# Squared-ReLU MLP of a two-layer decoder trunk: from column 1024 on, the up projection takes u's high and low part in one 512-column product

## Chip, cores and metric

One core of a Trainium2 chip. The metric is device time in microseconds (us) of one execution, lower is better.

## What is computed

Two decoder layers over 256 tokens of width 1024, all in f32. The change touches the second half of each layer, the MLP; from the reference:

```python
u = x * (1.0 + sc2) + sh2
h = jnp.square(jax.nn.relu(u @ w_up[l])) @ w_down[l]      # w_up 1024 x 4096, w_down 4096 x 1024
x = layer_norm(DN_ALPHA * x + (1.0 + gt2) * h, ln_ffn_g[l], ln_ffn_b[l])
```

`sc2`, `sh2`, `gt2` and their like for the first half come from `c_act @ w_ada[l] + b_ada[l]`, one row vector for all tokens.

## The kernel before

**Two-part products.** Every f32 operand of a large product is cut into a rounded high part and the rest (`wh`, `wl`; `uh`, `ul`; `hh`, `hl`), and a product is three matmuls into the same PSUM bank: high by high, high by low, low by high (`rowmm`, lines 312 to 316; `colmm`, lines 318 to 322). The first operand of a matmul call is the one that TensorE holds, the second streams through.

**Weights.** `Stream` (lines 101 to 147) loads all weights in units of 512 KB in the order of the list `units` (lines 278 to 300), with SP's queue into 5 raw tiles. ScalarE rounds a unit into `wh` (line 121), VectorE subtracts for `wl` (line 122). Eight units are live; the split of a new unit goes into the tiles of the unit that `done(i)` has just given up, so ScalarE's `wh` waits for TensorE's last product with that unit.

**The MLP** (`ffn`, lines 999 to 1057). Columns 0 to 1023 of the up projection go token by token row (`row_phase`). From column 1024 on it is done transposed, in blocks of 512 columns, b = 2 to 7: `col_group` holds a 128 x 128 piece of the weights and streams 256 tokens, 8 k-tiles x 4 column pieces x 3 products of 256 columns into the banks `ua` and `ub`; `relu2_split` then takes each bank out (ReLU, square, rounding on ScalarE, rest on VectorE) into `hid[b]`. Between two blocks stand 4 units of the down projection of the block before, 48 products of 512 columns into the four banks `acc`, which are called `d` in the profile. The last 8 units of the down projection follow, 48 products for each half of the tokens; behind each half come the norm and the next layer's `u`.

**Work beside it.** `Background.step()` is called after each unit and moves on, above all, the vectors from `w_ada`: on VectorE `adaa += ada * ccol` over 8 loads of 512 KB (`ada_dve_gate`, `ada_dve_cols`), three load tiles in turn. A gate vector is then spread over all rows (`gate_rows`, lines 436 to 449): ScalarE rounds (`gh`), VectorE subtracts (`gl`), TensorE multiplies with ones (`gtb`, line 445 with `gh`, line 446 with `gl`), for each half of 512 columns. In layer 0's MLP the gate rows of that layer and all of the next layer's shifts and scales run this way, in layer 1's only its last gate, in the first 12 us.

The order of instructions on each engine is fixed when the kernel is built, by a scheduler that starts from the order of the code; each engine works its list in order.

## Time and profile before

| | |
|---|---|
| median of 3 runs | 754.73 us (753.99 to 755.18) |
| the profiled execution's own time | 755.1 us |
| its span in the profile | 753.2 us |
| busy: TensorE / weight load / VectorE / ScalarE | 97% / 84% / 79% / 60% |
| granted TensorE clock, mean | 0.994 |

The profile is of one execution. Its span ends about 1.9 us short of that execution's own time. Busy shares are means over stages with different limits. PE is TensorE's products, PEld its weight loads, DVE VectorE, ACT ScalarE, SP the engine that issues the loads.

### The profile page before, as it was taken

Reading aid. Unit: us, or ns where it says so; the run is one execution under the profiler, and the core shown is the slowest. Engines: PE = TensorE matmul, PEld = TensorE weight load, DVE = VectorE, ACT = ScalarE, POOL = GpSimd, SP = SyncE. Lnnn points to the kernel's source line nnn. Section 1 sums busy time; section 2 is a strip of 40 time slices with the busy share of each in tenths; the row PEclk is TensorE's granted clock in tenths of the full one; section 3 lists DMA queues with packets and bytes.
Section 4 is the critical chain, followed back from the end, with each engine's and each line's share of the span. In section 5 each row is a group of like instructions: output and inputs, shape, how many; then the busy total and the mean of one; then the engine's idle time right before and its main releaser. Section 6 shows DMA issues by size and latency. Waiting matters only on the chain.

```text
span 753.2 us, 12252 instructions
## 1 busy us (share of the span) xinstructions
PE 733.7 (97%) x4648; PEld 633.3 (84%) x4648; DVE 592.7 (79%) x870; ACT 448.5 (60%) x737; POOL 15.0 (2%) x37
## 2 busy tenths in 40 slices
PE   6999999999999999999999999999999999999995
PEld 4667788899888999889877888899988889998885
DVE  2448999999798988688889999997879884454437
ACT  3439898875476654555454985976457565445530
POOL 0000000010000000000000000001000000000001
PEclk9999999999999999999999999999999999999998
DMA  9998889677368998899786744446546885555501
GB/s 278 310 326 318 312 306 321 230 255 247 132 228 276 398 395 319 313 319 343 265 304 218 268 131 161 142 146 212 193 158 221 292 308 179 194 196 189 176 1 56
DMA packets 81562, 181.40 MB, mean 241 GB/s; under 512 B 6264, under 2 KB 24544, under 8 KB 81504
## 3 DMA queue, kind: packets, MB, share of 16 engines
q1 hardware_dynamic: 81440, 180.61, 69.8%
q8 instruction: 36, 0.59, 0.3%
q14 instruction: 22, 0.18, 0.1%
q10 hardware_dynamic: 64, 0.02, 0.0%
HBM read 179.56 MB, written 1.05 MB: 240 GB/s over the span
## 4 chain that ended last, share of the span: by engine, by line
PE 84%; DMA 6%; DVE 4%; ACT 2%; issue 2%; SPq 1%; POOL 1%; POOLq 0%; DVEq 0%; ACTq 0%
PE d L315 6%; PE d L316 6%; PE d L314 6%; DMA ada<-in_w_ada_dram 4%; PE ua L320 3%; PE ua L322 3%; PE ua L321 3%; PE ub L321 3%; PE ub L320 3%; PE ub L322 3%; PE ga L320 2%; PE gb L320 2%; PE ga L321 2%; PE gb L321 2%; PE ga L322 2%; PE gb L322 2%
## 5 line engine op out<-in xcount | busy, mean ns | idle before, releaser
L121 ACT ACTIVATE wh<-w 128x1024 fp32r<-128x1024 f32 x232 | 244.7, 1059 | 190.5 <-PE d L316 58.3
L122 DVE TENSOR_TENSOR wl<-w,wh 128x1024 fp32r<-128x1024 f32 x232 | 281.7, 1224 | 87.3 <-ACT wh L121 86.5
L314 PE MATMUL d<-wh,hh 128*128 128x512 f32 (+1 forms) x256 | 99.6, 389 | 0.0
L315 PE MATMUL d<-wl,hh 128*128 128x512 f32 (+1 forms) x256 | 98.9, 386 | 0.0
L316 PE MATMUL d<-wh,hl 128*128 128x512 f32 (+1 forms) x256 | 98.9, 386 | 0.0
L604 DVE SCALAR_TENSOR_TENSOR acc<-hconv,vc,acc 128x256 f32<-128x256 f32 x150 | 65.8, 497 | 0.0
L314 PEld LDWEIGHTS d<-wh,hh 128*128 128x128 f32 x256 | 48.1, 188 | 10.1 <-ACT relusq L992 0.8
L316 PEld LDWEIGHTS d<-wh,hl 128*128 128x128 f32 x256 | 48.1, 188 | 9.8
L315 PEld LDWEIGHTS d<-wl,hh 128*128 128x128 f32 x256 | 48.1, 188 | 9.2
L320 PE MATMUL ua<-uh,wh 128*128 128x256 f32 x192 | 54.5, 284 | 0.0
L322 PE MATMUL ua<-uh,wl 128*128 128x256 f32 x192 | 54.3, 283 | 0.0
L320 PE MATMUL ub<-uh,wh 128*128 128x256 f32 x192 | 54.3, 283 | 0.0
L321 PE MATMUL ub<-ul,wh 128*128 128x256 f32 x192 | 54.3, 283 | 0.0
L322 PE MATMUL ub<-uh,wl 128*128 128x256 f32 x192 | 54.3, 283 | 0.0
L321 PE MATMUL ua<-ul,wh 128*128 128x256 f32 x192 | 54.3, 283 | 0.0
L600 ACT ACTIVATE tap<-hconv,vc 128x256 f32<-128x256 f32 x90 | 39.3, 501 | 0.1
L495 DVE SCALAR_TENSOR_TENSOR adaa<-ada,ccol,adaa 128x1024 f32<-128x1024 f32 x28 | 35.8, 1280 | 3.7 <-DMA ada<-in_w_ada_dram 3.6
L320 PEld LDWEIGHTS ua<-uh,wh 128*128 128x128 f32 x192 | 36.8, 192 | 1.3 <-issue 0.8
L320 PE MATMUL ga<-uh,wh 128*128 128x256 f32 x128 | 37.5, 293 | 0.0
L321 PEld LDWEIGHTS ua<-ul,wh 128*128 128x128 f32 x192 | 36.8, 192 | 0.4
L320 PE MATMUL gb<-uh,wh 128*128 128x256 f32 x128 | 36.9, 288 | 0.0
L320 PEld LDWEIGHTS ub<-uh,wh 128*128 128x128 f32 x192 | 36.9, 192 | 0.0
(274 smaller groups left out, 1704.4 us busy)
## 6 DMA issues: line engine op xcount, KB each, us to landing
ada<-in_w_ada_dram SPq DMA_DIRECT2D x80, 512.0 KB, 4.9
w<-in_w_in_dram SPq DMA_DIRECT2D x72, 512.0 KB, 4.8
w<-in_w_up_dram SPq DMA_DIRECT2D x64, 512.0 KB, 4.8
w<-in_w_down_dram SPq DMA_DIRECT2D x64, 512.0 KB, 5.2
ada<-in_w_ada_dram SPq DMA_DIRECT2D x32, 256.0 KB, 6.4
w<-in_w_out_dram SPq DMA_DIRECT2D x16, 512.0 KB, 4.3
w<-in_w_attn_br_dram SPq DMA_DIRECT2D x8, 512.0 KB
w<-in_w_conv_pw_dram SPq DMA_DIRECT2D x8, 512.0 KB, 4.8
```

Source lines behind the costliest of these rows:

```text
L121: a = nc.scalar.activation(wh, w, AF.Copy)
L122: b = nc.vector.tensor_tensor(wl, w, wh.bitcast(F32), op=ALU.subtract)
L314: nc.tensor.matmul(b, lh, wh, start=first, stop=False, skip_group_check=True)
L315: nc.tensor.matmul(b, lh, wl, start=False, stop=False, skip_group_check=True)
L316: return nc.tensor.matmul(b, ll, wh, start=False, stop=last, skip_group_check=True)
L320: nc.tensor.matmul(b, wh, rh, start=first, stop=False, skip_group_check=True)
L321: nc.tensor.matmul(b, wh, rl, start=False, stop=False, skip_group_check=True)
L322: nc.tensor.matmul(b, wl, rh, start=False, stop=last, skip_group_check=True)
L495: nc.vector.scalar_tensor_tensor(acc, src, ccol[:, j:j + 1], acc, op0=ALU.mult, op1=ALU.add)
L600: nc.scalar.activation(p[:, q % 2, :], hconv[:, q, j:j + S], AF.Copy, scale=w(j, q))
L604: nc.vector.scalar_tensor_tensor(acc[:, q, :], hconv[:, q, j:j + S], w(j, q), acc[:, q, :], op0=ALU.mult, op1=ALU.add)
```

## The change

Units of `w_up` from column 1024 on are 4 k-tiles x 256 columns instead of 2 x 512, so one row of a load is 1 KB and not 2 KB. The 6 blocks of 512 columns become 12 groups of 256, g = 4 to 15, each with 2 units of up and, up to g = 13, 2 units of down of group g - 2. `uh` and `ul` lie in one tile, so that a held `wh` piece streams both, 512 columns, into the two halves of one bank; `wl` streams `uh` alone, 256 columns, onto the first half. The piece f of 128 columns is now the outer loop: bank `ua` takes f = 0, `ub` f = 1. The two halves of a bank are added on the way out: ScalarE copies the second half, VectorE adds the first, and then (layer 0) ScalarE does ReLU and square, or (layer 1) VectorE does both in one pass.

```diff
-        for b in range(2, 8):
-            pair_units(w_up[l], 8, 512 * b)
-            row_units(w_down[l], 4 * (b - 1), 4, 0)
-        row_units(w_down[l], 28, 4, 0)
+        for b in range(4, 16):
+            for k in range(0, 8, 4):
+                units.append(w_up[l, k * 128:(k + 4) * 128, 256 * b:256 * b + 256].rearrange("(k p) n -> p k n", p=128))
+            if b < 14:
+                row_units(w_down[l], 2 * b - 4, 2, 0)
+        row_units(w_down[l], 24, 8, 0)
...
+        u = u_p.tile([128, 2, 2, KT, 128], F32R, name="u", tag="u")
+        return u[:, 0], u[:, 1], u.rearrange("p s h k t -> p (s h) k t")
...
+    def relu2_split(l, banks, hh, hl):
+
+        q = t_p.tile([128, 2, 256], F32, name="relusq", tag="t")
+        for f in range(2):
+            nc.scalar.activation(q[:, f], banks[f][:, 256:512], AF.Copy)
+            nc.vector.tensor_tensor(q[:, f], q[:, f], banks[f][:, 0:256], op=ALU.add)
+        if l:
+            nc.vector.scalar_tensor_tensor(q, q, 0.0, q, op0=ALU.max, op1=ALU.mult)
+        else:
+            nc.scalar.activation(q, q, AF.Relu)
+            nc.scalar.activation(q, q, AF.Square)
+        q = q.rearrange("p f (h t) -> p f h t", h=2)
+        nc.scalar.activation(hh, q, AF.Copy)
+        nc.vector.tensor_tensor(hl, q, hh.bitcast(F32), op=ALU.subtract)
...
-        for b in range(2, 8):
-            ids = ws.window(4)
+        for g in range(4, 16):
             ub = [bank("ua"), bank("ub")]
-            col_group(ids, lambda k: (uh[:, :, k, :], ul[:, :, k, :]), ub)
...
+            ids = ws.window(2)
+            for f in range(2):
+                fs = slice(128 * f, 128 * f + 128)
+                o = ub[f].rearrange("p (s t) -> p s t", s=4)
                 for n, i in enumerate(ids):
...
+                    for k in range(4):
+                        nc.tensor.matmul(o, wh[:, k, fs], u2[:, :, 4 * n + k, :], start=n == 0 and k == 0, stop=False,
+                                         skip_group_check=True)
+                        nc.tensor.matmul(o[:, 0:2], wl[:, k, fs], uh[:, :, 4 * n + k, :], start=False, stop=n == 1 and k == 3,
+                                         skip_group_check=True)
+                    if f:
+                        ws.done(i)
+                        bg.step()
...
+            relu2_split(l, ub, *(t[:, :, fs, :].rearrange("p h f t -> p f h t") for t in hid[g // 2]))
+            if g < 14:
+                down_group(g - 2)
```

The scheduler orders the engines anew. Three places matter below; in them `L1064` and `L1066` are the new products of 512 and 256 columns, `L1003` the new addition on VectorE, and the other lines those of before, moved down by 2 to 27.

**Place A, the first gate rows of layer 0's MLP.** TensorE before: they follow the last product of block 2.

```order
L321 MATMUL ub<-ul,wh_2766 128x256
L322 MATMUL ub<-uh,wl_2767 128x256
L445 MATMUL gtb<-gh,ones 128x512
L446 MATMUL gtb<-gl,ones 128x512
L445 MATMUL gtb<-gh,ones 128x512
L446 MATMUL gtb<-gl,ones 128x512
L314 MATMUL d_2796<-wh_2841,hh 128x512
L315 MATMUL d_2796<-wl_2842,hh 128x512
```

TensorE now: they stand between the down products of group 2 and the up products of group 5.

```order
L317 MATMUL d_2797<-wl_2765,hh 128x512
L318 MATMUL d_2797<-wh_2764,hl 128x512
L447 MATMUL gtb<-gh,ones 128x512
L448 MATMUL gtb<-gl,ones 128x512
L447 MATMUL gtb<-gh,ones 128x512
L448 MATMUL gtb<-gl,ones 128x512
L1064 MATMUL ua<-u,wh_2839 128x512
L1066 MATMUL ua<-u,wl_2840 128x256
```

VectorE before: both `gl` in one go, right behind the split of block 3's second unit.

```order
L495 SCALAR_TENSOR_TENSOR adaa_2770<-ada_2887,ccol,adaa_2770 128x1024
L122 TENSOR_TENSOR wl_2919<-w_2916,wh_2918 128x1024
L495 SCALAR_TENSOR_TENSOR adaa_2770<-ada_2922,ccol,adaa_2770 128x1024
L122 TENSOR_TENSOR wl_2952<-w_2949,wh_2951 128x1024
L442 TENSOR_TENSOR gl<-adaa_2770,gh 128x512 x2
L122 TENSOR_TENSOR wl_2984<-w_2981,wh_2983 128x1024
```

VectorE now: two additions, and one more split (`wl_2934`) ahead of the first `gl`, another (`wl_2965`) between the two.

```order
L497 SCALAR_TENSOR_TENSOR adaa_2768<-ada_2885,ccol,adaa_2768 128x1024
L1003 TENSOR_TENSOR relusq<-relusq,ua 128x256
L497 SCALAR_TENSOR_TENSOR adaa_2768<-ada_2920,ccol,adaa_2768 128x1024
L122 TENSOR_TENSOR wl_2917<-w_2914,wh_2916 128x1024
L122 TENSOR_TENSOR wl_2934<-w_2931,wh_2933 128x1024
L1003 TENSOR_TENSOR relusq<-relusq,ub 128x256
L444 TENSOR_TENSOR gl<-adaa_2768,gh 128x512
L122 TENSOR_TENSOR wl_2965<-w_2962,wh_2964 128x1024
L444 TENSOR_TENSOR gl<-adaa_2768,gh 128x512
```

On TensorE the gate rows moved behind one stretch of down products; on VectorE the second `gl` moved behind two more splits and two additions. ScalarE's `gh` for it now stands behind the split `wh_2964` and behind the ReLU of group 4, which reads both additions.

**Place B, the gate rows of layer 1's MLP.** TensorE before had the same four rows in one piece behind block 2. Now three stand ahead of group 5 and the fourth ahead of the last product of its first half:

```order
L317 MATMUL d_6429<-wl_6397,hh 128x512
L318 MATMUL d_6429<-wh_6396,hl 128x512
L447 MATMUL gtb<-gh,ones 128x512
L448 MATMUL gtb<-gl,ones 128x512
L447 MATMUL gtb<-gh,ones 128x512
L1064 MATMUL ua<-u,wh_6471 128x512
```

```order
L1066 MATMUL ua<-u,wl_6487 128x256
L1064 MATMUL ua<-u,wh_6486 128x512
L448 MATMUL gtb<-gl,ones 128x512
L1066 MATMUL ua<-u,wl_6487 128x256
L1064 MATMUL ub<-u,wh_6471 128x512
```

VectorE now, up to the second `gl`; before, both stood in one row behind the second of these splits, as at place A.

```order
L497 SCALAR_TENSOR_TENSOR adaa_6400<-ada_6552,ccol,adaa_6400 128x1024
L122 TENSOR_TENSOR wl_6549<-w_6546,wh_6548 128x1024
L122 TENSOR_TENSOR wl_6566<-w_6563,wh_6565 128x1024
L1003 TENSOR_TENSOR relusq<-relusq,ub 128x256
L444 TENSOR_TENSOR gl<-adaa_6400,gh 128x512
L1005 SCALAR_TENSOR_TENSOR relusq<-relusq 128x512
L122 TENSOR_TENSOR wl_6596<-w_6593,wh_6595 128x1024
L1011 TENSOR_TENSOR hl<-relusq,hh 128x2x2x128
L451 SCALAR_TENSOR_TENSOR gt_6569<-gtb,gt_6569 128x512
L122 TENSOR_TENSOR wl_6618<-w_6615,wh_6617 128x1024
L444 TENSOR_TENSOR gl<-adaa_6400,gh 128x512
```

Between the two `gl` lie now the ReLU pass of group 4, two splits, `hl` and one `gt`.

**Place C, the end of layer 0's MLP.** TensorE now does five down products of the last stretch between the two halves of group 15; before, no down product stood inside the last block.

```order
L1066 MATMUL ua<-u,wl_3827 128x256
L316 MATMUL d_2794<-wh_3861,hh 128x512
L317 MATMUL d_2794<-wl_3862,hh 128x512
L318 MATMUL d_2794<-wh_3861,hl 128x512
L316 MATMUL d_2795<-wh_3861,hh 128x512
L317 MATMUL d_2795<-wl_3862,hh 128x512
L1064 MATMUL ub<-u,wh_3805 128x512
L1066 MATMUL ub<-u,wl_3806 128x256
```

VectorE before, from the last split but one to the norm's first row `ygt`; `adaa_4231` is the next gate's sum, over `ada_4250` (its third load), `ada_4259`, `ada_4268` and `ada_4337` (its sixth).

```order
L122 TENSOR_TENSOR wl_4183<-w_4180,wh_4182 128x1024
L996 TENSOR_TENSOR hl<-relusq,hh 128x2x2x128 x2
L495 SCALAR_TENSOR_TENSOR adaa_4231<-ada_4250,ccol,adaa_4231 128x1024
L480 TENSOR_TENSOR adac_148<-adat_4225,vc_2324 128x16
L495 SCALAR_TENSOR_TENSOR adaa_4231<-ada_4259,ccol,adaa_4231 128x1024
L578 SCALAR_TENSOR_TENSOR G<-adac_148,vc_2324 128x8
L579 SCALAR_TENSOR_TENSOR B<-adac_148,vc_2324 128x8
L495 SCALAR_TENSOR_TENSOR adaa_4231<-ada_4268,ccol,adaa_4231 128x1024
L580 TENSOR_TENSOR B<-B,adac_148 128x8
L495 SCALAR_TENSOR_TENSOR adaa_4231<-ada_4337,ccol,adaa_4231 128x1024
L543 TENSOR_TENSOR ygt<-d_2796,gt_2955 128x512
```

VectorE now, from the addition of group 15's second bank on; the norm's `ygt` follows right behind the last row, the sixth load.

```order
L1003 TENSOR_TENSOR relusq<-relusq,ub 128x256
L493 TENSOR_SCALAR adaa_4085<-ada_4086,ccol 128x1024
L497 SCALAR_TENSOR_TENSOR adaa_4085<-ada_4095,ccol,adaa_4085 128x1024
L482 TENSOR_TENSOR adac_148<-adat_4079,vc_2323 128x16
L497 SCALAR_TENSOR_TENSOR adaa_4085<-ada_4104,ccol,adaa_4085 128x1024
L1011 TENSOR_TENSOR hl<-relusq,hh 128x2x2x128
L582 SCALAR_TENSOR_TENSOR G<-adac_148,vc_2323 128x8
L583 SCALAR_TENSOR_TENSOR B<-adac_148,vc_2323 128x8
L584 TENSOR_TENSOR B<-B,adac_148 128x8
L497 SCALAR_TENSOR_TENSOR adaa_4085<-ada_4113,ccol,adaa_4085 128x1024
L497 SCALAR_TENSOR_TENSOR adaa_4085<-ada_4122,ccol,adaa_4085 128x1024
L497 SCALAR_TENSOR_TENSOR adaa_4085<-ada_4190,ccol,adaa_4085 128x1024
```

The third load's pass moved from behind both `hl` to behind that addition and two more passes; the chain from there to `ygt` kept its form.

## Rows read from the trace of the kernel before

**Rows 1.** The page, part 1: busy us, share, instructions.

```profile
PE 733.7 (97%) x4648; PEld 633.3 (84%) x4648; DVE 592.7 (79%) x870; ACT 448.5 (60%) x737; POOL 15.0 (2%) x37
```

**Rows 2.** Busy by stretch, up projection of layers 0, 1; last: clock, DMA share, GB/s.

```profile
243.30:369.50 126.20, 126.20 (x833) 115.33 (x832) 104.53 (x101) 64.51 (x78) 0.00 (x0) 1.00 0.92 339
598.50:724.50 126.00, 126.00 (x828) 116.05 (x827) 69.03 (x64) 65.27 (x79) 0.00 (x0) 1.00 0.57 195
```

**Rows 3.** Timeline of TensorE (start, duration): 15 products apart, then 39 products apart.

```profile
239.70 0.39 PE L316 MATMUL d<-wh,hl 128*128 128x512 f32 x1
...
243.10 0.39 PE L316 MATMUL d<-wh,hl 128*128 128x512 f32 x1
...
243.44 0.28 PE L321 MATMUL ua<-ul,wh 128*128 128x256 f32 x1
...
248.12 0.28 PE L321 MATMUL ua<-ul,wh 128*128 128x256 f32 x1
```

**Rows 4.** Tile ua: number, ns min/median/max of its products and its way out.

```profile
L320 PE MATMUL ua<-uh,wh x192: 277/283/386, 243.3 to 722.0; 128*128 128x256 f32 x192
...
L990 ACT ACTIVATE relu<-ua x12: 574/597/601, 254.8 to 722.6; 128x512 f32<-128x512 f32 x12
```

**Rows 5.** Instructions that read 256 columns of PSUM: line 732; timeline of VectorE.

```profile
L732 ACT ACTIVATE gth<-glu x4: 386/396/413, 407.1 to 419.8; 128x256 f32<-128x256 f32 x4
```

```profile
734.80 0.41 DVE L1129 TENSOR_TENSOR ygt<-d,gt 128x256 f32<-128x256 f32 x1
```

**Rows 6.** Timeline of ScalarE, start of layer 0's up projection; in brackets the idle time.

```profile
251.84 1.06 ACT L121 ACTIVATE wh<-w 128x1024 fp32r<-128x1024 f32 x1 [1.59 <-DMA w<-in_w_up_dram]
252.81 1.14 ACT L441 ACTIVATE gh<-adaa 128x512 fp32r<-128x512 f32 x2
```

**Rows 7.** Timeline of VectorE and of TensorE at the gate rows, layer 0.

```profile
251.43 1.28 DVE L495 SCALAR_TENSOR_TENSOR adaa<-ada,ccol,adaa 128x1024 f32<-128x1024 f32 x1
...
254.08 1.29 DVE L442 TENSOR_TENSOR gl<-adaa,gh 128x512 fp32r<-128x512 f32 x2
```

```profile
254.84 0.40 PE L445 MATMUL gtb<-gh,ones 128*128 128x512 f32 x1
```

**Rows 8.** Timeline of ScalarE, VectorE and TensorE at the gate rows, layer 1.

```profile
606.95 1.06 ACT L121 ACTIVATE wh<-w 128x1024 fp32r<-128x1024 f32 x1 [1.60 <-DMA w<-in_w_up_dram]
```

```profile
601.88 2.35 DVE L122 TENSOR_TENSOR wl<-w,wh 128x1024 fp32r<-128x1024 f32 x2
604.15 1.28 DVE L495 SCALAR_TENSOR_TENSOR adaa<-ada,ccol,adaa 128x1024 f32<-128x1024 f32 x1
...
609.18 1.29 DVE L442 TENSOR_TENSOR gl<-adaa,gh 128x512 fp32r<-128x512 f32 x2
```

```profile
598.52 0.28 PE L320 MATMUL ua<-uh,wh 128*128 128x256 f32 x1
...
610.03 0.40 PE L445 MATMUL gtb<-gh,ones 128*128 128x512 f32 x1
```

**Rows 9.** TensorE's first down product behind layer 0's up projection, and its wait at the next u.

```profile
369.51 0.40 PE L314 MATMUL d<-wh,hh 128*128 128x512 f32 x1
```

```profile
390.13 1.08 PE L368 MATMUL utr<-ident,xall 128*128 128x128 f32 x8 [0.38 <-DVE xall L555]
```

**Rows 10.** The chain of work that ended last, end of layer 0 (start, us, what).

```profile
374.17 1.28 DVE adaa L495
375.48 4.77 DMA ada<-in_w_ada_dram
380.35 1.28 DVE adaa L495
381.63 1.37 DVE ygt L543 x2
```

**Rows 11.** DMA of two full stretches, 12 to 54 us and 255 to 277 us.

```profile
DMA packets 16868, 13.20 MB, mean 314 GB/s; under 512 B 982, under 2 KB 15133, under 8 KB 16866
```

```profile
DMA packets 2914, 8.76 MB, mean 398 GB/s; under 512 B 267, under 2 KB 267, under 8 KB 2912
```

More of the change, by code (lines that the diff above doesn't have):

```diff
@@ L513, in u_tiles @@
     def u_tiles():
-        return (u_p.tile([128, 2, KT, 128], F32R, name="uh", tag="uh"), u_p.tile([128, 2, KT, 128], F32R, name="ul", tag="ul"))
+        u = u_p.tile([128, 2, 2, KT, 128], F32R, name="u", tag="u")
+        return u[:, 0], u[:, 1], u.rearrange("p s h k t -> p (s h) k t")
     def make_u(u, h, G, B, at):
-        uh, ul = u
+        uh, ul, _ = u
         for c in range(2):
@@ L740, in first_proj @@
     def first_proj(u):
-        uh, ul = u
+        uh, ul, _ = u
         bk = [[bank(f"p{n}{h}") for n in range(3)] for h in range(2)]
@@ L851, in mixer @@
     def mixer(l, u):
-        uh, ul = u
+        uh, ul, _ = u
         lhs = lambda n, h: (uh[:, h, n, :], ul[:, h, n, :])
@@ L992, in relu2_split @@
         nc.scalar.activation(q, r, AF.Square)
-        if hh is not None:
-            q = view(q)
-            nc.scalar.activation(hh, q, AF.Copy)
-            nc.vector.tensor_tensor(hl, q, hh.bitcast(F32), op=ALU.subtract)
-        return q
+        return q
+    def relu2_split(l, banks, hh, hl):
[11 more added lines that the diff above has]
+        nc.vector.tensor_tensor(hl, q, hh.bitcast(F32), op=ALU.subtract)
     def ffn(l, u):
-        uh, ul = u
+        uh, ul, u2 = u
         lhs = lambda n, h: (uh[:, h, n, :], ul[:, h, n, :])
@@ L1013, in ffn @@
             for c in range(2):
-                q = relu2_split(b[c], None, None, None)
+                q = relu2(b[c])
                 ts = []
@@ L1021, in ffn, with down, down_group @@
         acc = [[bank("d00"), bank("d01")], [bank("d10"), bank("d11")]]
-        def down(b):
-            return lambda n, h: (hid[b][0][:, h, n, :], hid[b][1][:, h, n, :])
+        def down(g):
+            return lambda n, h: (hid[g // 2][0][:, h, 2 * (g % 2) + n, :], hid[g // 2][1][:, h, 2 * (g % 2) + n, :])
+        def down_group(g):
+            for n, i in enumerate(ws.window(2)):
+                wh, wl = ws.live[i]
+                for h in range(2):
+                    lh, ll = down(g)(n, h)
+                    for c in range(2):
+                        cs = slice(512 * c, 512 * c + 512)
+                        rowmm(acc[h][c], lh, ll, wh[:, cs], wl[:, cs], False, False)
+                ws.done(i)
+                bg.step()
@@ L1026, in ffn @@
         ids = ws.window(4)
         for h in range(2):
-            row_phase(ids, h, down(0), acc[h], first=True, last=False, release=h == 1)
-        for b in range(2, 8):
-            ids = ws.window(4)
+            row_phase(ids, h, lambda n, h: down(n // 2)(n % 2, h), acc[h], first=True, last=False, release=h == 1)
+        for g in range(4, 16):
             ub = [bank("ua"), bank("ub")]
-            col_group(ids, lambda k: (uh[:, :, k, :], ul[:, :, k, :]), ub)
-            hid_tiles(b)
-            for i in range(2):
-                fs = slice(2 * i, 2 * i + 2)
-                relu2_split(ub[i], hid[b][0][:, :, fs, :].rearrange("p h f t -> p f h t"),
-                            hid[b][1][:, :, fs, :].rearrange("p h f t -> p f h t"),
-                            lambda q: q.rearrange("p (f h t) -> p f h t", f=2, h=2))
-            if b < 7:
-                ids = ws.window(4)
-                for n, i in enumerate(ids):
-                    wh, wl = ws.live[i]
-                    for h in range(2):
-                        lh, ll = down(b - 1)(n, h)
-                        for c in range(2):
-                            cs = slice(512 * c, 512 * c + 512)
-                            rowmm(acc[h][c], lh, ll, wh[:, cs], wl[:, cs], False, False)
-                    ws.done(i)
-                    bg.step()
@@ new lines, in ffn @@
+            ids = ws.window(2)
+            for f in range(2):
+                fs = slice(128 * f, 128 * f + 128)
+                o = ub[f].rearrange("p (s t) -> p s t", s=4)
+                for n, i in enumerate(ids):
+                    wh, wl = (w.rearrange("p (k n) -> p k n", k=4) for w in ws.live[i])
+                    for k in range(4):
[4 more added lines that the diff above has]
+                    if f:
+                        ws.done(i)
+                        bg.step()
@@ L1050, in ffn @@
+            if g % 2 == 0:
+                hid_tiles(g // 2)
+            fs = slice(2 * (g % 2), 2 * (g % 2) + 2)
+            relu2_split(l, ub, *(t[:, :, fs, :].rearrange("p h f t -> p f h t") for t in hid[g // 2]))
+            if g < 14:
+                down_group(g - 2)
         ids = ws.window(8)
-        both = lambda n, h: down(6 + n // 4)(n % 4, h)
+        both = lambda n, h: down(12 + n // 2)(n % 2, h)
         for h in range(2):
```

2 lines of the change are left out of this document (1 added, 1 removed).

## The prediction

> **What bounds the kernel now.** I read the page's busy shares first: TensorE is busy 97% of the span [rows 1]. A mean can hide stages, so I then read the two up-projection stretches by window. TensorE is busy in all 126.2 us of layer 0's and all 126.0 us of layer 1's, at granted clock 1.00, which is the level of 2.4 GHz [rows 2]. Time taken from TensorE there is time won, unless a wait appears. VectorE is busy 104.5 us in layer 0's stretch (83%) and 69.0 in layer 1's, ScalarE 64.5 and 65.3, and the DMA engines 0.92 and 0.57 of the time [rows 2]. So layer 0 has little room on VectorE and the DMA, layer 1 has much. Third, the chain of waits at the end of layer 0's MLP: for 12 us it doesn't run over TensorE, but over VectorE's sums for the next gate, one load of 4.77 us, and then `ygt` [rows 10]; TensorE waits 0.38 us at the next `u` [rows 9].
>
> **What the change removes.** From the timeline, 512-column products follow each other at (243.10 - 239.70)/15 = 226.7 ns and 256-column products at (248.12 - 243.44)/39 = 120.0 ns [rows 3]. Columns at 2.4 GHz take 213.3 and 106.7 ns of that, so each product costs 13.3 ns beside its columns, whatever its length. Three products of 256 took 360.0 ns; a pair of 512 and 256 takes 226.7 + 120.0 = 346.7. The columns are the same 768; what is won is one product's 13.3 ns. `ua` had 192 products with `uh` and `wh` in both layers [rows 4], so with `ub` there are 384 triples, 192 per layer: 384 x 13.3 ns = **5.1 us**, 2.56 per layer. Nothing else is taken from TensorE.
>
> Here the Trainium skill, page "TensorE: Matmul & The Clock Gate", section "Back-to-back issue gap", states another price: a product's isolated spacing is its columns at 2.4 GHz plus about 2.5 ns. By it 384 products fewer would be worth an estimated 1.0 us. The trace disagrees with the 2.5 ns: it has 13.3 at both lengths.
>
> **What it adds off TensorE.** Per group, ScalarE gets two copies of 256 PSUM columns and VectorE two additions; the nearest rows, same shapes, are 0.40 us on ScalarE and 0.41 on VectorE [rows 5]. Layer 0: 24 x 0.40 = 9.5 us on ScalarE, 24 x 0.41 = 9.8 on VectorE, which goes to about 114 of 124 us. Layer 1: ReLU and square move to VectorE, 12 passes of about 0.65, so VectorE goes from 69 to about 87. By share all of it is hidden behind TensorE: a bank that is read has the 5.44 us of the 24 down products (24 x 226.7 ns) and half a group (8 x 346.7 = 2.77) until it is needed. If that cover were gone, a group would pay its way out, about 2 us. But the queues are in order, and at three places the additions come ahead of something that TensorE waits for. There I lay out the new order by the old durations.
>
> *Place A* (layer 0). ScalarE's `wh` that waits for its load at 251.84 [rows 6] is `wh_2933`, and it stays at that load's time. It ends at 252.9. VectorE: `wl_2934` to 254.1, `ub`'s addition to 254.45, first `gl` to 255.05. ScalarE: `wh_2964`, then group 4's ReLU, which waits for the addition, then the second `gh` to about 255.7 (half of 1.14, [rows 6]). VectorE: `wl_2965` to 256.2, second `gl` to 256.8 (half of 1.29, [rows 7]). TensorE comes there at 243.33 + 16 x 0.3467 + 24 x 0.2267 = 254.32 and would be through the four gate rows at 255.25; with the last row at 256.95 it starts group 5 at 257.2, **2.0 us late**. Before, the rows ran at 254.84, where TensorE came anyway [rows 7]. Behind the fourth row stand all up products. Bounds: 0 (`gl` ready in time) to 3 (one more split and ReLU ahead of it).
>
> *Place B* (layer 1), the same with one more thing in the queue: `wh` at 606.95 by its load [rows 8], `wl_6566` to 609.15 (a split takes 1.14, from [rows 8]: two from 601.88 to 604.15), addition 609.55, first `gl` 610.15. TensorE is there at 598.52 + 5.55 + 5.44 + 0.23 = 609.74: **0.6 late** with the first wait and its row. Then the ReLU pass, `wl_6596`, `hl`, `gt` and `wl_6618` bring the second `gl` to about 614.85; TensorE, by then in the last product of group 5's first half, is there at about 613.5: **1.4 late**. Before, both `gl` were done at 610.47 and the rows at 610.03 cost nothing [rows 8]. Together 2.0; bounds 0 to 3.
>
> *Groups 14 to 15* have no down products between them. In layer 0 `ub`'s way out is queued behind a split and a sum (1.26 + 1.14 + 1.2 + 0.4 = 4.0 us) against 2.77 + 1.13 of cover: 0.1 to 0.4, I take 0.25. In layer 1, 0.2 on the same working (bounds 0 to 0.5).
>
> *Place C* (end of layer 0). Before, from the last up product (369.51, [rows 9]) to `ygt` (381.63, [rows 10]) are 12.1 us, set by the gate's loads. The third load's pass frees the tile that the sixth load goes to. Now: `ub`'s way out and a split, 1.26 + 1.14 + 0.35 = 2.75, two passes and small work up to the end of the third pass 6.1, load 4.77 to 10.9, last pass 1.28 to 12.2. So the chain is as long as before and hangs on the same point; but the five hoisted down products, 5 x 0.2267 = 1.13 us, now lie in front of that point instead of beside the chain: **+1.1**, as a longer wait at `utr` (about 2 us instead of 0.38). Bounds 0 (the pass comes first) to 2.3 (it comes one pass later).
>
> Units are cut differently too, rows of 1 KB for 2 KB. The number of units is the same. Two full stretches bound it: 314 GB/s where nine packets in ten are under 2 KB, 398 where nine in ten are between 2 and 8 KB [rows 11]. For 512 KB that is 1.67 us against 1.32: 0 to 0.35 per unit. The slow stretch is the start of the kernel with other loads in it, so it is far; I take 0 for the sum and keep 0.35 for the range.
>
> The Trainium skill, page "DMA: Bandwidth & Descriptors", section "Specifications", asks for at least 512 B in a transfer for full rate, so by it 1 KB rows cost nothing. No row of this trace has w_up in 1 KB rows, so it can't be held against it.
>
> **Sum**, against the profiled execution's 755.1 us: -5.1 + 2.0 + 2.0 + 0.25 + 0.2 + 1.1 = +0.45, so 755.55. That execution lies 0.4 above the median of the runs, 754.73, so on the median **755.2 us**. What this kernel's measurement can tell from no change is about 0.2%, 1.5 us: same.
>
> **Rivals.**
> 1. *Faster: the gate rows don't wait.* It decides whether the second `gl` ends before TensorE is through with the rest, 255.0 at place A and 613.5 at place B. For it: the misses are 1 to 2 us in orders laid out by hand over a dozen steps, and one load that lands a microsecond earlier takes most of them away. Against: the load that ScalarE waits for is in the trace at both places (1.59 and 1.60 us, [rows 6, 8]). Then 4.0 us fall away: 755.2 - 4.0 = 751.2.
> 2. *Slower: loads of 1 KB rows cost more.* 24 units x 0.35 = 8.4 us more load time in a stretch of 126 whose DMA share is 0.92, which is 10 us free. For it: the 314 GB/s. Against: that stretch is another one. The loads at places A and B and the load of place C would come about 0.7 later each, two units behind, and that is paid three times: 755.2 + 2.1 = 757.3. It decides from about 0.2 us per unit.
> 3. *The change doesn't do what it says*: the 13.3 ns goes with what streams, one share for each run of 128 or 256 columns, so that a product over two tiles' worth of `u` costs 240 and not 226.7 ns. Then the 5.1 us are not won: 755.2 + 5.1 = 760.3. Against it: the 512-column down products, which stream one run of `hh`, give no hint either way, but 120.0 for 256 columns that come from two pieces of 128 is on the same line with 226.7.
> Beside this rival stands the price of the page on TensorE: with 1.0 us won instead of 5.1 the time would be 759.3. The trace's two spacings speak against it.
>
> **Chances.** The forecast 0.50, its own range 753.5 to 756.6 (one place misjudged by 1.5 us either way); rival 1 0.27; rival 2 0.18; rival 3, either price, 0.05. The range 751.0 to 758.0 leaves out about a third of rival 1 (0.10), a quarter of rival 2 (0.05) and rival 3 (0.05), 2 in 10. Against 754.73 +- 1.5: faster is 0.25 of rival 1 and 0.03 of the forecast, 0.28; slower 0.14 of rival 2, 0.05 of rival 3 and 0.05 of the forecast, 0.24; same is the rest, 0.48.
>
> **What would show it.** In the profile after: 384 TensorE products fewer; 346.7 ns from pair to pair; waits of TensorE of about 2 us at the fourth `gtb` in layer 0, 0.6 and 1.4 in layer 1, put down to VectorE's `gl`; 0.2 us at the second half of group 15; about 2 us at `utr` behind layer 0's MLP; VectorE's layer-0 stretch about 114 us. If the waits at `gtb` are missing, rival 1 is right. If `wh` waits longer for w_up's loads throughout layer 0, and DMA rate falls well under 339 GB/s there, it is rival 2. If the pair's spacing isn't 346.7, the first term is wrong. What would upset all: VectorE in layer 0, at 92%, falling behind group after group, so that TensorE waits for `wl` in every block.

## The result, and the profile after

The changed kernel is slower: median 760.6 us (8 runs, 758.73 to 762.12) against 755.93 us for the kernel before in the same set of runs, a ratio of 1.0056, 95% interval [1.0031, 1.0081]. Its profiled execution took 760.41 us, 5.2 more than the profiled one of before (755.18). The forecast was 755.2 and "same", with a range of 751.0 to 758.0.

The page, part 1, of the kernel after (busy us, share, instructions):

```profile
PE 733.6 (97%) x4264; PEld 612.9 (81%) x4264; DVE 618.4 (82%) x930; ACT 452.3 (60%) x761; POOL 15.0 (2%) x37
```

The 384 products fewer are there (4648 in [rows 1]), and TensorE is as busy as before. The two up-projection stretches by window (PE, PEld, DVE, ACT, POOL busy; then clock, DMA share, GB/s):

```profile
242.42:372.27 129.85, 128.49 (x646) 107.14 (x645) 112.67 (x125) 74.17 (x103) 0.00 (x0) 0.99 0.92 327
602.37:728.41 126.04, 123.88 (x630) 104.50 (x628) 84.76 (x99) 60.86 (x80) 0.00 (x0) 1.00 0.60 195
```

Against [rows 2], TensorE is now idle 1.4 us in layer 0's stretch and 2.2 in layer 1's, and layer 0's clock is not 1.00 throughout. (Layer 0's stretch now holds 1.15 us of hoisted down products.) TensorE's timeline in group 4, the first product and the first one behind the 16 pairs:

```profile
242.42 0.39 PE L1064 MATMUL ua<-u,wh 128*128 128x512 f32 x1
...
248.06 0.40 PE L316 MATMUL d<-wh,hh 128*128 128x512 f32 x1
```

16 pairs take 5.64 us, 352.5 ns a pair, and so in nearly every group of both layers. The forecast had 346.7 from [rows 3]. TensorE's waits that the forecast spoke of, over the whole span (total, times, longest):

```profile
PE gtb L448 <- DVE gl L444: 3.4, 4, 1.2
...
PE utr L370 <- DVE xall L559: 2.2, 4, 1.4
```

*Place A.* TensorE at layer 0's gate rows, in brackets its idle time, and the first products behind:

```profile
253.54 0.39 PE L447 MATMUL gtb<-gh,ones 128*128 128x512 f32 x1
254.54 0.49 PE L448 MATMUL gtb<-gl,ones 128*128 128x512 f32 x1 [0.62 <-DVE gl L444]
255.12 0.51 PE L447 MATMUL gtb<-gh,ones 128*128 128x512 f32 x1
256.28 0.50 PE L448 MATMUL gtb<-gl,ones 128*128 128x512 f32 x1 [0.65 <-DVE gl L444]
256.62 0.55 PE L1064 MATMUL ua<-u,wh 128*128 128x512 f32 x1
...
258.46 0.63 PE L1064 MATMUL ua<-u,wh 128*128 128x512 f32 x1
...
259.10 0.63 PE L1064 MATMUL ua<-u,wh 128*128 128x512 f32 x1
```

Four gate rows from 253.54 to 256.62 are 3.08 us, where they took 0.94 from 254.84 on before ([rows 7]): **2.1 us**, as forecast. What was not forecast stands right behind: pairs 0.64 us apart at 258.46. The same place by windows (the column behind the zeros of POOL is the granted clock):

```profile
254.00:256.00 2.00, 1.00 (x2) 0.37 (x2) 2.00 (x3) 1.97 (x4) 0.00 (x0) 1.00 1.08 376
256.00:258.00 2.00, 1.72 (x6) 1.48 (x7) 2.00 (x4) 1.21 (x2) 0.00 (x0) 0.68 1.08 372
258.00:260.00 2.00, 2.00 (x8) 1.71 (x7) 2.00 (x4) 0.00 (x0) 0.00 (x0) 0.50 1.04 408
260.00:262.00 2.00, 2.00 (x12) 1.71 (x12) 0.89 (x2) 0.39 (x1) 0.00 (x0) 0.97 1.03 408
```

The clock is down to 0.50, the level of 1.2 GHz, after the half-idle 2 us from 254, and back by about 260. Group 5 takes 7.13 us (256.62 to 263.75) instead of 5.64: **1.5 us** more.

*Place B.* The gate rows in layer 1:

```profile
613.48 0.39 PE L447 MATMUL gtb<-gh,ones 128*128 128x512 f32 x1
614.79 0.50 PE L448 MATMUL gtb<-gl,ones 128*128 128x512 f32 x1 [0.92 <-DVE gl L444]
...
615.36 0.39 PE L1064 MATMUL ua<-u,wh 128*128 128x512 f32 x1
...
617.82 0.40 PE L1064 MATMUL ua<-u,wh 128*128 128x512 f32 x1
619.46 0.50 PE L448 MATMUL gtb<-gl,ones 128*128 128x512 f32 x1 [1.24 <-DVE gl L444]
```

Three rows would end 0.68 us behind 613.48, but group 5 starts at 615.36 (1.2 late), and group 5 with the fourth row runs to 622.75, 7.39 us where 5.64 + 0.23 were due, 1.5 more: **2.7 us**. The granted clock stayed at 1.00 here.

*Place C.* The chain of work at the end of layer 0's MLP, and TensorE's next product that needs it:

```profile
377.20 1.29 DVE adaa L497
378.50 5.46 DMA ada<-in_w_ada_dram
384.06 1.29 DVE adaa L497
385.34 1.20 DVE ygt L547 x2
```

```profile
393.66 0.52 PE L370 MATMUL utr<-ident,xall 128*128 128x128 f32 x3 [1.37 <-DVE xall L559]
```

The same chain as in [rows 10], with a load of 5.46 us instead of 4.77. The last up product ends at 372.27. From there to `utr` are 21.4 us, 20.6 before ([rows 9]), and 1.15 us of down products lie ahead of it now: **1.9 us**.

**The account of the two profiled executions**, from the first up product of layer 0 (243.3 before, 242.4 after) to the span's end (753.2 and 758.5), 509.9 and 516.1 us, 6.2 more: 24 groups x (5.64 - 5.76) = -2.8; place A 2.1 and the clock behind it 1.5; place B 2.7; place C 1.9; group 14 to 15 0.2; 20 down stretches at 5.47 instead of 24 x 0.2272 = 5.45, 0.3; the mixer behind layer 0's MLP 0.3. Together 6.2. What lies before that (0.9 shorter here) the change doesn't touch.

### The profile page after: what moved, and what is told of

Read it like the earlier page. It is cut to its first block, busy times and chain, and to the rows that moved or that the text cites. A ratio compares the mean times of both kernels' runs of the same rounds, so it can differ in the third digit from the quotient of the medians.

```text
span 758.5 us, 11568 instructions
## 1 busy us (share of the span) xinstructions
PE 733.6 (97%) x4264; PEld 612.9 (81%) x4264; DVE 618.4 (82%) x930; ACT 452.3 (60%) x761; POOL 15.0 (2%) x37
## 4 chain that ended last, share of the span: by engine, by line
PE 68%; DVE 12%; DMA 9%; issue 3%; ACT 3%; SPq 3%; POOL 1%; POOLq 0%; DVEq 0%; ACTq 0%
PE ub L1064 5%; PE d L316 5%; PE d L317 5%; PE ua L1064 5%; PE d L318 5%; DMA ada<-in_w_ada_dram 4%; DVE wl L122 4%; PE ub L1066 3%; PE ua L1066 3%; DMA w<-in_w_up_dram 2%; PE ga L322 2%; PE gb L322 2%; PE ga L323 2%; PE gb L323 2%; PE ga L324 2%
## 5 line engine op out<-in xcount | busy, mean ns | idle before, releaser
L1064 PE MATMUL ua<-u,wh 128*128 128x512 f32 x192 | 70.2, 404 | 0.0
L1064 PE MATMUL ub<-u,wh 128*128 128x512 f32 x192 | 69.3, 400 | 0.0
L1066 PE MATMUL ua<-u,wl 128*128 128x256 f32 x192 | 54.5, 284 | 0.0
L1066 PE MATMUL ub<-u,wl 128*128 128x256 f32 x192 | 53.9, 281 | 0.0
L1064 PEld LDWEIGHTS ua<-u,wh 128*128 128x128 f32 x192 | 36.8, 192 | 9.7 <-issue 0.8
L1064 PEld LDWEIGHTS ub<-u,wh 128*128 128x128 f32 x192 | 36.1, 188 | 9.2 <-DVE relusq L1003 0.5
L1066 PEld LDWEIGHTS ua<-u,wl 128*128 128x128 f32 x192 | 37.0, 193 | 0.8
L322 PE MATMUL ga<-u,wh 128*128 128x256 f32 x128 | 37.5, 293 | 0.0
L322 PE MATMUL gb<-u,wh 128*128 128x256 f32 x128 | 36.9, 288 | 0.0
L323 PE MATMUL ga<-u,wh 128*128 128x256 f32 x128 | 36.8, 288 | 0.0
L324 PE MATMUL gb<-u,wl 128*128 128x256 f32 x128 | 36.4, 284 | 0.0
```

The costliest lines, as they stand in the source:

```text
L322: nc.tensor.matmul(b, wh, rh, start=first, stop=False, skip_group_check=True)
L323: nc.tensor.matmul(b, wh, rl, start=False, stop=False, skip_group_check=True)
L324: nc.tensor.matmul(b, wl, rh, start=False, stop=last, skip_group_check=True)
L1064: nc.tensor.matmul(o, wh[:, k, fs], u2[:, :, 4 * n + k, :], start=n == 0 and k == 0, stop=False, skip_group_check=True)
L1066: nc.tensor.matmul(o[:, 0:2], wl[:, k, fs], uh[:, :, 4 * n + k, :], start=False, stop=n == 1 and k == 3, skip_group_check=True)
```

## The experiments

Each was profiled, and those with an interval were timed against the kernel before. Times of one run alone say little here, since the kernel before ran from 754 to 760 us; the stretches in the profiles say more.

**e1, u in one run.** Two theories of why a pair takes 352.5 and not 346.7 ns: the 512 columns of `u` lie in four pieces, or the lengths change from product to product.

```diff
-        u = u_p.tile([128, 2, 2, KT, 128], F32R, name="u", tag="u")
-        return u[:, 0], u[:, 1], u.rearrange("p s h k t -> p (s h) k t")
+        u = u_p.tile([128, KT, 2, 2, 128], F32R, name="u", tag="u")
+        v = u.rearrange("p k s h t -> p s h k t")
+        return v[:, 0], v[:, 1], u.rearrange("p k s h t -> p (s h) k t")
```

> The changed kernel with u stored by k-tile, so that the 512 columns that a held wh streams (and the 256 that wl streams) lie in one run instead of four (two) runs of 128 that are 4 KB apart; nothing else moves. In the changed kernel 16 pairs take 5.64 us, 352.5 ns a pair. Theory A, the streamed operand's pieces cost the missing 5.8 ns: 16 pairs take 5.55 us or less, the 24 groups together lose 2.2 us or more, the time goes 2.2 us below the changed kernel's, at the same waits. Rival B, the change of length from product to product costs it, or what is written into the bank: 16 pairs stay at 5.64 us and the time stays.

Measured: 762.63 us, ratio 1.0074 [1.0049, 1.0098]. TensorE's timeline, first product of a group and the first behind it:

```profile
327.15 0.39 PE L1065 MATMUL ua<-u,wh 128*128 128x512 f32 x1
...
332.79 0.40 PE L316 MATMUL d<-wh,hh 128*128 128x512 f32 x1
```

5.64 us as before. The pieces cost nothing: theory A falls. (The wait at place A was 2.9 us in this run, and the clock fell to 0.50 there too.)

**e2, gate rows later.** The products of the MLPs' gate rows are issued by a generator of their own, four steps behind `gh` and `gl` instead of half a step; the sums for the next vectors keep their times.

```diff
-        for c in range(2):
-            yield from gate_rows(t, c, ones, acc[:, 512 * c:512 * c + 512])
-            yield 0.0
+        def rows(lag):
+            for c in range(2):
+                yield from gate_rows(t, c, ones, acc[:, 512 * c:512 * c + 512], lag)
+                yield 0.0
+
+        r = rows(4.0 if v == 5 else GATE_LAG)
+        if v == 5:
+            bg.add(r, next(r))
...
```

> The changed kernel with only the products of the MLPs' gate rows put later in the order: two in the middle of the down products behind group 5, two in the middle of those behind group 6. Theory, their place cost it: TensorE's waits at gtb there vanish (2.1 us in layer 0, 1.2 and 1.6 in layer 1), the stretch at granted clock 0.50 behind the wait in layer 0 vanishes too (1.5 us in group 5), and the time goes 6 us below the changed kernel's. Rival, VectorE and the loads are late by themselves and the wait only moves on, to wl or to the banks: groups 5 and 6 together keep at least 3 of the 6 us, as waits at another line. If the clock falls for another reason than the wait, 0.50 shows again near 257 us.

Measured: 756.22 us, ratio 0.9989 [0.9972, 1.0007]; span 754.0 instead of 758.5. TensorE at the first two rows:

```profile
262.82 0.39 PE L447 MATMUL gtb<-gh,ones 128*128 128x512 f32 x1
263.05 0.39 PE L448 MATMUL gtb<-gl,ones 128*128 128x512 f32 x1
263.28 0.40 PE L316 MATMUL d<-wh,hh 128*128 128x512 f32 x1
```

No idle time, every group 5.64 us, granted clock 1.00 through both up projections. The waits did not move on. From the first up product to the span's end it is 5.4 us shorter than the changed kernel (754.0 - 243.3 = 510.7 against 516.1).

**e3, lengths grouped by unit**, and **e7, by bank half.** The 512-column products ahead of the 256-column ones, four and four, then eight and eight (e7's loops; in e3 only the loop over k is cut in two).

```diff
-                for n, i in enumerate(ids):
-                    wh, wl = (w.rearrange("p (k n) -> p k n", k=4) for w in ws.live[i])
-                    for k in range(4):
-                        nc.tensor.matmul(o, wh[:, k, fs], u2[:, :, 4 * n + k, :], ...
-                        nc.tensor.matmul(o[:, 0:2], wl[:, k, fs], uh[:, :, 4 * n + k, :], ...
+                ws4 = [[w.rearrange("p (k n) -> p k n", k=4) for w in ws.live[i]] for i in ids]
+                for k in range(8):
+                    nc.tensor.matmul(o, ws4[k // 4][0][:, k % 4, fs], u2[:, :, k, :], ...
+                for k in range(8):
+                    nc.tensor.matmul(o[:, 0:2], ws4[k // 4][1][:, k % 4, fs], uh[:, :, k, :], ...
```

> The changed kernel with the 8 products of a unit's half in another order: first the four of 512 columns, then the four of 256. Theory B, the alternation of lengths (a weight load that has only 256 columns to hide behind, ahead of a product of 512) costs 5.8 ns a pair: 16 pairs go from 5.64 to about 5.57 us, as three of four changes of length are gone. Theory A, the pieces cost it: 5.64 us stay.

> The changed kernel with all eight 512-column products of a half group ahead of its eight 256-column ones. 16 pairs took 5.64 us with 16 changes from 256 to 512, 5.585 with four in 16; without any such cost they would take 16 x 346.7 = 5.547. If the cost is one of the change of length, two changes in 16 give 5.56 to 5.57. If a part of it belongs to the 512-column products over four pieces, or to their bank, 5.585 stays.

TensorE's timeline of a group in e3, and in e7 (x8 are eight products in one row):

```profile
328.57 1.07 PE L1064 MATMUL ua<-u,wh 128*128 128x512 f32 x4
...
334.16 0.40 PE L316 MATMUL d<-wh,hh 128*128 128x512 f32 x1
```

```profile
324.12 1.98 PE L1063 MATMUL ua<-u,wh 128*128 128x512 f32 x8
325.93 1.12 PE L1066 MATMUL ua<-u,wl 128*128 128x256 f32 x8
326.88 2.00 PE L1063 MATMUL ub<-u,wh 128*128 128x512 f32 x8
328.73 1.11 PE L1066 MATMUL ub<-u,wl 128*128 128x256 f32 x8
...
329.68 0.40 PE L316 MATMUL d<-wh,hh 128*128 128x512 f32 x1
```

5.59 us with four returns to 512 in 16 pairs, 5.56 with two, 5.64 with 16; the reckoning from [rows 3] without any such price is 5.547. So nearly all that was missing goes with the change of length, and rival B holds. It is not one price for each return: in e7 the eight products of 512 columns behind the return took 1.85 us (326.88 to 328.73), the first eight of the group 1.81. And one group does without it. In e4 (below), which changes nothing here, the alternating pairs of layer 0's group 5 stand behind the wait at place A, at granted clock 1.00:

```profile
258.61 0.40 PE L1068 MATMUL ua<-u,wh 128*128 128x512 f32 x1
...
264.16 0.39 PE L316 MATMUL d<-wh,hh 128*128 128x512 f32 x1
```

These 16 pairs took 5.55 us. The second half of group 5 in the changed kernel, behind the half-speed stretch, took 2.77 us for 8 pairs, without the price too; the same group in e5 took 5.65. What the price hangs on beside the order of lengths stays open. In single runs e3 took 761.62 us, e7 757.09; the clock stayed at 1.00 at place A in both.

**e8, two of 256.** The fused product alone taken back.

```diff
-                        nc.tensor.matmul(o, wh[:, k, fs], u2[:, :, 4 * n + k, :], ...
+                        nc.tensor.matmul(o[:, 0:2], wh[:, k, fs], uh[:, :, 4 * n + k, :], ...
+                        nc.tensor.matmul(o[:, 2:4], wh[:, k, fs], ul[:, :, 4 * n + k, :], ...
```

> The changed kernel with the fused product alone taken back: wh streams uh and ul in two products of 256 columns into the two halves of the bank; groups, loads, additions and gate rows stay. Theory, the fusion is worth 7.5 ns a triple: 16 triples take 5.76 us instead of 5.64, 24 groups 2.9 us, and everything else (waits at gtb of about 2 and 2.8 us, 21 us from the last up product to utr) stays as in the changed kernel. Rival, the forecast's 13.3 ns were right and something else in the changed kernel stretches all products: then 16 triples take 5.85.

```profile
326.93 0.28 PE L1064 MATMUL ua<-u,wh 128*128 128x256 f32 x1
...
332.68 0.40 PE L316 MATMUL d<-wh,hh 128*128 128x512 f32 x1
```

5.75 us for 16 triples, 0.11 more than with pairs: 24 groups, 2.7 us. That is what the fused product is worth in the alternating order. The run took 760.57 us, no more than the changed kernel's profiled one: here the clock stayed at 1.00 at place A, and the stretch from the last up product to `utr` was 20.4 us, so the rest did not stay as it was, as the expectation had it.

**e4, no hoist.** The last stretch's down products ordered behind the last up product.

```diff
-            row_phase(ids, h, both, acc[h], first=False, last=True, release=h == 1)
+            row_phase(ids, h, both, acc[h], first=False, last=True, release=h == 1, behind=up)
...
+        for i in m:
+            order(i, behind)
```

> The changed kernel with the last stretch's down products of layer 0 held behind its last up product, so that none stands between the halves of group 15. Theory, the five hoisted products lie ahead of the chain of the next gate's sum instead of beside it: from group 15's first product to the first utr behind layer 0's MLP the time falls by 1.0 to 1.2 us, and up to 0.2 comes back as a wait at group 15's second half. Rival, the chain doesn't hang on the end of the up products but on its own loads: the stretch keeps its length within 0.3 us.

The scheduler put products of the next vectors (`adar`) into the gap instead, and these waited. One of TensorE's waits near the end of layer 0's MLP:

```profile
PE adar L479 <- DVE adaa L474: 0.7, 1, 0.7
```

From group 15's first product to `utr` 28.7 us, against 28.3 in the changed kernel. The stretch did not shorten, but group 15 itself took 7.5 us, where 5.8 were due without down products in it, and from the last up product to `utr` are 21.2 us, as in the changed kernel (21.4). Something else had come into the stretch, so this run decides nothing.

**e9, longer wait.** The last `gl` computed twice, group 5 and the down products behind it held behind the last gate row.

```diff
-            nc.vector.tensor_tensor(lo, e, hi.bitcast(F32), op=ALU.subtract)
+            for _ in range(late):
+                nc.vector.tensor_tensor(lo, e, hi.bitcast(F32), op=ALU.subtract)
...
+                        if (l, g, f, n, k) == (0, 5, 0, 0, 0):
+                            order(m, last_gt[0])
```

> The changed kernel with the last gl of layer 0's MLP made later on VectorE (it is computed twice; a sum, hl, gt and a split come to stand ahead of the second time, 3.8 us by their rows), and group 5 and the down products behind it held behind the gate rows' last product, so that TensorE waits longer there. In the runs so far TensorE waited 2.0 to 2.9 us at this place: behind 2.1 and 2.9 the granted clock showed 0.50 and group 5 took 7.1 and 6.8 us, behind 2.0 to 2.1 in five others it stayed 1.00 and group 5 took 5.6 to 5.75. Theory, the wait brings the clock down: a wait of 5 to 6 us, then 0.50, and group 5 at about 7.1 us. Rival, the clock fell for another reason in those two runs: group 5 at 5.64 with granted clock 1.00. Beside it, as none of the last down products stands between the halves of group 15 here: the time from group 15's first product to the first utr behind layer 0's MLP is 1.0 to 1.2 us shorter than in the changed kernel if the chain of the next gate's sum hangs on the end of the up products.

TensorE at the gate rows, and the windows behind:

```profile
258.88 0.79 PE L453 MATMUL gtb<-gl,ones 128*128 128x512 f32 x1 [4.26 <-DVE gl L449]
259.47 0.63 PE L1069 MATMUL ua<-u,wh 128*128 128x512 f32 x1
...
267.28 0.40 PE L316 MATMUL d<-wh,hh 128*128 128x512 f32 x1
```

```profile
257.00:259.00 2.00, 0.12 (x1) 0.12 (x1) 2.00 (x4) 0.00 (x0) 0.00 (x0) 0.61 1.06 403
259.00:261.00 2.00, 2.00 (x6) 1.71 (x7) 1.18 (x2) 0.00 (x0) 0.00 (x0) 0.50 1.01 404
```

The four gate rows take 6.77 us (252.70 to 259.47) instead of 0.94, so the wait in all is 5.8 us. The clock falls while it lasts, and group 5 takes 7.81 us, 2.2 more than 5.64. The wait brings the clock down; with e2, where there is neither wait nor drop, that is shown from both sides, in one profile each. In this run (763.73 us) no down product stands inside group 15, and from its first product to `utr` are 28.6 us, again not shorter. But here a seventh pass, with a wait for its load, stands ahead of `ygt`, where the changed kernel has six:

```profile
387.95 1.29 DVE L502 SCALAR_TENSOR_TENSOR adaa<-ada,ccol,adaa 128x1024 f32<-128x1024 f32 x1 [1.81 <-DMA ada<-in_w_ada_dram]
```

So neither e4 nor e9 decides what the five hoisted products cost.

**e5, norm first.** Sixth to eighth pass of the next gate's sum behind the norm.

```diff
+            while (l, v) == (1, 2) and j == 5 and not normed:
+                yield 0.5
...
+                if (l, v, j) == (1, 2, 5):
+                    order(i, normed[0])
```

> The changed kernel with the sixth, seventh and eighth pass of the next gate's sum, and their loads, put behind the norm of the first token half at the end of layer 0's MLP; nothing else is meant to move. Theory, ygt there waits for the third pass, one load and the sixth pass (13.1 us from the end of the up products to ygt, with the five hoisted products ahead of them): with the norm first, ygt starts when TensorE is through with the first token half, 383.7 in the changed kernel's trace instead of 385.3, and the time from the end of the up products to the first utr falls from 21.4 us to about 19.7. Rival, VectorE is late by itself or the load of the next weights is what counts: less than 0.5 us falls, or it comes back as a wait in the next mixer.

VectorE's last pass and `ygt`:

```profile
380.83 1.28 DVE L499 SCALAR_TENSOR_TENSOR adaa<-ada,ccol,adaa 128x1024 f32<-128x1024 f32 x1 [1.42 <-DMA ada<-in_w_ada_dram]
382.03 1.37 DVE L551 TENSOR_TENSOR ygt<-d,gt 128x512 f32<-128x512 f32 x2
```

The last up product ends at 371.02, so `ygt` starts 11.0 us behind it instead of 13.0, and `utr` 19.3 instead of 21.4. 2.1 us are won up to there; 1.3 come back ahead of the next mixer's first `q` (30.7 us from `utr` to it instead of 29.4). One run, 758.24 us.

**e10, way out twice.** On top of e2, every copy and addition of the banks' way out done twice.

```diff
-            nc.scalar.activation(q[:, f], banks[f][:, 256:512], AF.Copy)
-            nc.vector.tensor_tensor(q[:, f], q[:, f], banks[f][:, 0:256], op=ALU.add)
+            for _ in range(2):
+                nc.scalar.activation(q[:, f], banks[f][:, 256:512], AF.Copy)
+                nc.vector.tensor_tensor(q[:, f], q[:, f], banks[f][:, 0:256], op=ALU.add)
```

> The kernel with later gate rows, with each copy and each addition of the way out done twice (48 more of 0.4 us on ScalarE and on VectorE, half of them in each layer); the result is the same. The forecast cost this work at nothing where it lies beside TensorE. Theory, that holds, with the banks' 8 us of cover: layer 1's 12 groups keep 11.1 us a pair of up and down, and layer 0's lose at most 1 us in all. Rival, VectorE in layer 0 is at its limit (it was busy 110 of 126 us in the changed kernel, 10 more are 120): waits for wl or for a bank show from group to group, 3 us or more in layer 0.

TensorE waits for that work twice, once in each layer (over the whole span), and VectorE is busy 119.2 of 127.7 us in layer 0's stretch:

```profile
PE ua L1074 <- DVE relusq L1013: 0.8, 2, 0.5
```

```profile
243.43:371.13 127.70, 127.33 (x650) 106.63 (x649) 119.19 (x147) 81.48 (x126) 0.00 (x0) 1.00 0.95 333
```

Both waits are at the start of group 5. Even at double price the added work is hidden elsewhere (one run, 756.03 us).

**e6, e11 and e12: what a repaired version is worth.** e6 has e2, e7 and e5 together, e11 e2 and e7, e12 is the kernel before with e5's edit alone.

> The changed kernel with three repairs: the products of the MLPs' gate rows later, all eight 512-column products of a half group ahead of its eight 256-column ones, and the next gate's last three passes behind the norm. Theory, what the changed kernel loses is these three places: 6.2 us (gate rows with the clock), about 1.7 (alternation of lengths, two changes in 16 products instead of 16: 16 pairs at 5.57 us), 1.7 (norm), so 9.5 us below the changed kernel and 4 to 5 below the kernel before, a ratio of about 0.994. Rival, the repairs only move waits: a ratio of 0.998 or more.

> The changed kernel with later gate rows and grouped lengths, without the change at the norm. Of the 2.1 us that the norm's place won up to utr, 1.3 came back in the next mixer, so 0.8 are its net worth. Theory: this kernel is 0.5 to 1.0 us above the one with all three, a ratio to the kernel before of 0.996 to 0.997. Rival, the norm's place is worth all of its 2.1 us: a ratio of 0.998.

> The kernel before with the next gate's last three passes behind the norm of layer 0's first token half, the one of the three repairs that does not belong to the change. In the trace of before ygt starts 12.1 us behind the last up product, and TensorE itself is through with the first token half about then. Theory: nothing to win there, within 0.3 us, and up to 1.2 comes back in the next mixer as it did in the changed kernel: a ratio of 1.000 to 1.002, so that what the kernel with the three repairs wins (0.9956) belongs to the fused product. Rival, the repair is worth as much to the kernel before: a ratio of 0.997 to 0.998, and about half of that gain has nothing to do with the change.

| | us, median | ratio to before | interval |
|---|---|---|---|
| e6, gate rows, lengths, norm | 753.23 | 0.9956 | 0.9935 to 0.9976 |
| e11, gate rows, lengths | 754.53 | 0.9977 | 0.9960 to 0.9994 |
| e12, before with norm first | 756.89 | 1.0011 | 0.9992 to 1.0029 |

e6 beats both kernels, by 0.44% and, by the two ratios, about 1%; that is 3.3 us below the kernel before where 4 to 5 were expected. e12 shows why the norm's repair has nothing to give before the change: with the passes moved away `ygt` starts 12.1 us behind the last up product, no earlier than before, and now waits for TensorE.

```profile
381.98 1.37 DVE L547 TENSOR_TENSOR ygt<-d,gt 128x512 f32<-128x512 f32 x2 [3.36 <-PE d L316]
```

So there is something to win only where the passes are later than TensorE, as in the changed kernel. The intervals of e6 and e11 overlap; what the norm's place nets (0.8 expected, 1.6 by the two ratios) is not settled.

## Why the prediction was wrong

**The saving per product failed, in its size.** "What is won is one product's 13.3 ns", 5.1 us: it measured 2.8 in the changed kernel, and 2.7 with the fusion alone taken back (e8). The two spacings of [rows 3] were read from stretches where the length does not change, and the sum took them as prices of single products. Where 512 and 256 alternate, about 6 ns a pair come on top in nearly every group; grouped, the 346.7 come back to within 1 ns (e7), and 24 x (5.76 - 5.56) = 4.8 us are won, close to the forecast. Why the alternation costs this, and did not in e4's group 5, is not shown.

Rival 3 asked whether 13.3 ns go with the pieces that stream: no. In one run or in four pieces a pair takes the same (e1), and in e7 eight products over four pieces follow each other at 1.81/8 = 0.227 us. That its 760.3 lies close to the measured 760.6 is chance. The 1.0 us estimated from the Trainium skill ("TensorE: Matmul & The Clock Gate", "Back-to-back issue gap"), whose 2.5 ns are for an isolated product, were too little by 1.7 to 1.8 us, where the forecast's 5.1 were too much by 2.3 to 2.4.

**Place A was right, and its consequence was missing.** 2.1 us measured, 2.0 forecast, for the reason given: the second `gl` behind an addition, a split and a `gh` that waits for the ReLU. Rival 1, no waits at the gate rows, falls with it. But the forecast priced a wait of TensorE as its own length. It can cost the clock too: 1.5 us of 3.6 in the profiled execution. In their profiles the same place waited 2.0 to 2.1 us in five kernels (e3, e4, e5, e7, e8) without a drop, and what decides at this length is not shown.

The median hardly has this drop in it. The profiled execution's mean granted clock is 0.995. Eight profiles (e2, e4, e5, e7, e8, e10, e11, e12), which have no half-speed stretch between the start and the end, show 0.996 to 0.998, and the six profiles with one show 0.994 or 0.995. Six of the changed kernel's eight runs have 0.997 or 0.998, so they very likely had no drop. These six took 758.73 to 762.12 us. Without the 1.5 us the account comes to 4.7, which is how far the two medians lie apart (760.6 - 755.93).

**Place B** was right in its working: 2.7 measured against 2.0, the fourth row 1.5 late and the first three 1.2 instead of 1.4 and 0.6. The working held ScalarE's `wh` at the time that its load had before. In the profile after, the same `wh` at places A and B:

```profile
251.24 1.06 ACT L121 ACTIVATE wh<-w 128x1024 fp32r<-128x1024 f32 x1 [1.43 <-DMA w<-in_w_up_dram]
```

```profile
611.48 1.06 ACT L121 ACTIVATE wh<-w 128x1024 fp32r<-128x1024 f32 x1 [1.43 <-DMA w<-in_w_up_dram]
```

Counted from the layer's first up product (242.42 and 602.37) these are 8.8 and 9.1 us, where [rows 6] and [rows 8] have 8.5 and 8.4. The 0.7 us at place B are what the forecast lacks there. At place A little is left of the 0.3, as TensorE came 0.1 later itself. In the other profiles with 1 KB rows this time lies between 8.3 and 9.6 us, and e12, with 2 KB rows, has 9.2 and 8.5, so it moves without the change too.

**Place C** came out as a loss of 1.9 instead of 1.1. The chain that the forecast laid out is in the trace, third pass, load, sixth pass, `ygt`, and `utr` follows `ygt` by 8.3 to 8.5 us in every profile. What was mis-sized is the load, taken at the 4.77 of [rows 10], where it took 5.46: 0.7 of the missing 0.8. That the other 1.15 us come from the hoisted products is argued and not shown, since e4 and e9 decide nothing. In the eight profiles after the change that have six passes ahead of `ygt`, it starts 11.9 to 13.9 us behind the last up product, on the whole the later the longer these passes waited for their loads (0.9 to 3.0 us in all). What makes those loads land early or late stays open.

**Hidden work stayed hidden**: VectorE is busy 112.7 us in layer 0's stretch (114 forecast) and 84.8 in layer 1's (87), and doubling it cost two waits, 0.8 us in all (e10). Group 14 to 15 gave 0.1 in each layer.

**Rival 2: its price is not there.** Two windows of the same stretch with the DMA engines full, 248 to 262 us, after and before:

```profile
DMA packets 2659, 5.51 MB, mean 393 GB/s; under 512 B 171, under 2 KB 1701, under 8 KB 2657
```

```profile
DMA packets 1935, 5.64 MB, mean 403 GB/s; under 512 B 172, under 2 KB 172, under 8 KB 1933
```

The first window has 1530 packets of 1 KB (1701 - 171), three units' worth, and its rate is 2.5% lower. 5.51 MB take 0.35 us longer at 393 than at 403 GB/s, so an estimate is about 0.1 us for a unit of 512 KB, not 0.35, and under the 0.2 from which the rival was to decide. Rows under 2 KB alone don't explain the slow 314 GB/s of [rows 11]. Layer 0's whole stretch has 327 GB/s instead of 339, about the same bytes (42.5 and 42.7 MB) in 3.6 us more, and TensorE's only waits in it are the two at `gtb`. Still, the loads at places A, B and C came 0.3, 0.7 and 0.7 us later than the forecast took them, near to the 0.7 each that the rival named. With the spread of these loads over the profiles, their rows are not shown to be the reason.

The Trainium skill ("DMA: Bandwidth & Descriptors", "Specifications") asks for at least 512 B in a transfer for full rate, by which 1 KB rows cost nothing. The trace about agrees: the estimated 0.1 us is small beside the 1.3 us that 512 KB take at these rates.

So the sign came from 2.3 us of saving too much and from 0.7 to 0.8 each at places B and C, where a load came 0.7 us later than the row of before; in the profiled execution 1.5 of a clock that was not priced come on top.

## What to carry to other kernels

A spacing read from a run of equal instructions is not the price of one of them in a mix: look for a stretch that alternates, or keep equal lengths together. When a change lengthens the way out of a bank, follow what stands behind the new instructions in each queue up to the next product that waits, because the work itself may be free while its place costs microseconds. A wait of TensorE can cost more than its length: look at the granted clock of the products behind it, and in more than one execution, before its price goes into an account. Where a forecast holds a load at its old time, give it the spread that this time has over several profiles.

## Not expected of the hardware

- Products of 512 columns behind products of 256 were slower than among themselves: one for one, 16 pairs took 5.64 us, grouped by eight 5.56, and in e7 eight of them took 1.85 us behind a return and 1.81 without one. In e4's group 5, behind a wait of TensorE, 16 alternating pairs took 5.55.
- Four strided pieces of 128 columns streamed as fast as one run of 512: 5.64 us for 16 pairs both ways.
- The granted clock fell to 0.50 behind waits of 2.1, 2.9 and 5.8 us in a stretch that was otherwise full, and stayed at 1.00 behind five of 2.0 to 2.1. The delays of 1.2 and 1.5 us at place B, four microseconds apart, brought no drop.
